# Gates applied on the way out of PSUM, and expert results summed by accumulating transfers, in a two-block MoE and hybrid-layer kernel

## The chip, the cores and the metric

One core of one Trainium2 chip runs the whole program in one launch. The metric is device time in microseconds (us), the median of several executions; the kernel before has 2867.81 us over three runs (2863.91 to 2868.19). The engines are called PE (matmul), PEld (weight load, beside PE), DVE, ACT, POOL and SP, as in the profile; each works through its own queue in order. SP's queue carries only transfers; POOL's and ACT's carry transfers beside their arithmetic.

## The reference

Two transformer blocks run one after the other on 512 tokens of width 1024. The first ends in a mixture of experts: each token goes to its 4 best of 32 experts, and the 4 results are weighted by softmax gates and summed. The second block is a hybrid layer (two attentions, a state-space branch, a gated convolutional feed-forward) which begins with a normalisation of the first block's output.

```python
gate = jax.nn.softmax(top_val, axis=-1)          # of the 4 best of 32 logits
def expert_block(args):
    gu = xblk @ w_gu[e] + b_gu[e]
    act = (up + 1.0) * (g * jax.nn.sigmoid(SWIGLU_ALPHA * g))   # after clamps
    return act @ w_down[e] + b_down[e]
out = zeros.at[tok_buf].add(yb * w_buf[:, None])               # w_buf: the gates
...
h = h + g2 * rmsnorm(ff, ffn_post_g)             # end of the first block
h = modulate(rms_norm(x, norm1), shift1, scale1) # start of the second
```

Since the gates of a token enter linearly, b_down can be summed apart, as gates times b_down, and each expert's result can be scaled by its gate at any place before the sum.

## The kernel before, in words

Every product is computed in three passes (each operand is split into a high and a low part), so that each 512 KB piece of weights is loaded by SP (`Stream.load`, L1541, tile `raw`), rounded by ACT (`hi`, L1566), subtracted by DVE or POOL (`lo`, L1568), and then streamed through PE (L1225 for the experts, L135 to L137 and L1719 elsewhere). Few `raw` buffers exist: SP's next load waits until DVE has read the buffer that it reuses.

The stages that the change touches, in order of time:

1. **Router** (`router`, L1025 to L1100, about 379 to 393 us). It computes ranks, gates G (128 x 4 x 32) and the table TW, which holds for each token and expert the four numbers that a slot of an expert's block must learn: token number (two columns), a one, and the token's choice number 0 to 3. At its end (L1096 to L1099) eight DVE instructions pick the four gates of each token into `k.gk`.
2. **Slots** (`make_slots`, L1150 to L1173). A one-hot matrix times TW puts the four numbers of each token into the slot that it has in the expert's block (L1162); DVE turns them into row numbers for the gather of the tokens (L1195) and for the scatter of the results (L1279). It runs for expert 0 first, and later for groups of up to four experts beside the experts' products. `further` (L1319) does the same for one block that is found at run time.
3. **Experts** (`experts`, `go_on`, about 410 to 1620 us). The loop over 32 experts is written out by hand for PE, ACT, DVE and POOL. For each of its 33 blocks of 128 rows, `out` (L1272) copies two 128 x 512 results from PSUM to `ey` on ACT (L1277), and POOL scatters the rows to `y_d` in HBM (L1279), at row 4 x token + choice.
4. **Middle** (`mid`, L2757 to L2802, about 1606 to 1686 us). PE multiplies the gates by b_down and ACT copies the sums to `xn` (L2779, L2780). Then for each of four token tiles: four fetches of 512 KB from `y_d` into `my` (L2786, on POOL's queue, 5 buffers), each added with its gate to `xn` by DVE (L2787); then the norm (ACT L2791, DVE L149, POOL L152, DVE L2793), the residual (DVE L2794), a store of it (POOL L2795), and the second block's norm (ACT L2796, POOL L152, ACT L2798). `run` (L2563) weaves this generator with `J.ctx`, the products of the 256 context tokens, whose weights come from `w_in` by SP; the numbers that the generators yield set how much of `J.ctx` is written between their steps.
5. **Turned** (`turned_g`, L1763). PE transposes the finished `xn` (L1770, four tiles into one bank, so that it needs all four), and then come the large products of the second block.

From the middle on, only the program order is written by hand; the framework lists each engine's instructions by when their inputs are ready in its own plan. The trace shows this: POOL issues the fetches of tile 1 before tile 0's power operation, which stands ahead of them in the program. On the chip each queue then runs in that fixed order.

Of the kernel before, what the change touches and what calls it, by code (L numbers as in the profile page):

```python
# [10 lines left out]
F32 = mybir.dt.float32  # L11
F32R = mybir.dt.float32r
BF16 = mybir.dt.bfloat16
I32 = mybir.dt.int32
AF = mybir.ActivationFunctionType
OP = mybir.AluOpType
AX = mybir.AxisListType
# [3 lines left out]
P = 128  # L21
D = 1024
T = 512
NT = T // P
# [5 lines left out]
TOPK = 4  # L30
# [994 lines left out]
def router(k, A, pool, lg, counted):  # L1025

    nc = k.nc
    TT = lambda o, a, b, op: nc.vector.tensor_tensor(o, a, b, op=op)
    E = NE
# [2 lines left out]
    ub = pool.tile([P, 2, P], BF16, name="ub")  # L1032
    nc.gpsimd.tensor_copy(ub[:, 0, :], k.C("upper"))
    nc.gpsimd.memset(ub[:, 1, :], 1.0)
    k.TW = k.mk.tile([P, NT, E, 4], BF16, name="TW")
    TW = k.TW
    nc.gpsimd.tensor_copy(TW[:, :, :, 0], k.C("p").unsqueeze(2).to_broadcast(sh))
    for t in range(NT):
# [11 lines left out]
    inc = pool.tile(sh, F32, name="rinc")  # L1050
# [15 lines left out]
    ps = sm_ps(k)  # L1066
# [14 lines left out]
    num = pool.tile(sh, F32, name="rnum")  # L1081
# [5 lines left out]
    G = pool.tile(sh, F32, name="G")  # L1087
# [5 lines left out]
    nc.vector.reciprocal(gs, gs)  # L1093
    TT(G, G, gs.unsqueeze(2).to_broadcast(sh), OP.mult)

    k.gk = lg[:, :, :TOPK]  # L1096
    for i in range(TOPK):
        nc.vector.scalar_tensor_tensor(inc, num, float(i), G, op0=OP.is_equal, op1=OP.mult)
        nc.vector.tensor_reduce(k.gk[:, :, i], inc, axis=AX.X, op=OP.add)  # L1099
    return G  # L1100


# [12 lines left out]
class Experts:  # L1115
# [34 lines left out]
    def make_slots(s, key, ranks, tw, n):  # L1150

        k, nc, pool = s.k, s.nc, s.pool
        oh = pool.tile([P, NT, n, P], BF16, name="oh", tag="oh", bufs=1)
        for t in range(NT):
            nc.vector.tensor_tensor(oh[:, t], s.iota.unsqueeze(1).to_broadcast([P, n, P]),
                                    ranks[:, t].unsqueeze(2).to_broadcast([P, n, P]), op=OP.is_equal)
            if t % 2:
                yield 1.5
        ps = sm_ps(k)
        for e in range(n):  # L1160
            for t in range(NT):
                nc.tensor.matmul(ps[:, e * 4:(e + 1) * 4], oh[:, t, e, :], tw(t, e), start=(t == 0), stop=(t == NT - 1))  # L1162
        yield 0.5
        sl = pool.tile([P, n, 4], F32, name="slots", tag="slots", bufs=2)
        nc.vector.tensor_copy(sl, ps[:, :4 * n].rearrange("p (e c) -> p e c", e=n))
        TT = lambda o, a, b, op: nc.vector.tensor_tensor(o, a, b, op=op)
        TT(sl[:, :, 0], sl[:, :, 0], sl[:, :, 1], OP.add)
        nc.vector.tensor_scalar(sl[:, :, 1], sl[:, :, 2], k.C("mdummy"), k.C("dummy"), op0=OP.mult, op1=OP.add)
        TT(sl[:, :, 1], sl[:, :, 1], sl[:, :, 0], OP.add)
        nc.vector.scalar_tensor_tensor(sl[:, :, 3], sl[:, :, 1], float(TOPK), sl[:, :, 3], op0=OP.mult, op1=OP.add)  # L1170
        idx = pool.tile([P, n, 2], I32, name="idx", tag="idx", bufs=3)
        nc.vector.tensor_copy(idx, sl[:, :, 1::2])
        s.groups[key] = [(idx[:, e, 0:1], idx[:, e, 1:2]) for e in range(n)]  # L1173

    def slots_g(s, i):

# [95 lines left out]
    def out(s, b, step=None):  # L1272
        nc = s.nc
        if step in (0, None):
            b.y = s.pool.tile([P, D], F32, name="ey", tag="ey", bufs=1)
            for n in range(2):
                nc.scalar.copy(b.y[:, n * 512:(n + 1) * 512], b.pd[n])  # L1277
        if step in (1, None):
            nc.gpsimd.indirect_dma_start(out=s.k.y_d[:, :], out_offset=bass.IndirectOffsetOnAxis(ap=b.slot[1], axis=0),  # L1279
                                         in_=b.y, in_offset=None, bounds_check=TOPK * T - 1, oob_is_err=False)  # L1280
# [38 lines left out]
    def further(s, i, b):  # L1319

        k, nc, pool = s.k, s.nc, s.pool
        TT = lambda o, a, b, op: nc.vector.tensor_tensor(o, a, b, op=op)
# [4 lines left out]
        oh = pool.tile([P, NE], F32, name="exoh", tag="exoh", bufs=1)  # L1327
# [4 lines left out]
        nc.vector.tensor_reduce(rk, tmp, axis=AX.X, op=OP.add)  # L1332
        nc.vector.tensor_scalar(rk, rk, ecol[:, 1:2], None, op0=OP.subtract)
        yield 1.0
        tw = pool.tile([P, NT, 4], BF16, name="extw", tag="extw", bufs=1)
        for c in range(4):
            TT(tmp, k.TW[:, :, :, c], oh.unsqueeze(1).to_broadcast(sh), OP.mult)
            with nc.allow_low_precision("one term is not zero"):
                nc.vector.tensor_reduce(tw[:, :, c:c + 1], tmp, axis=AX.X, op=OP.add)
# [449 lines left out]
class Block2:  # L1789
# [967 lines left out]
    def mid(s):  # L2757

        k, nc = s.k, s.nc
# [15 lines left out]
        for t in range(NT):  # L2775
            for n in range(2):
                c = slice(n * 512, (n + 1) * 512)
                ps = sm_ps(k)
                nc.tensor.matmul(ps, gT[:, t * P:(t + 1) * P], bd[:, c], start=True, stop=True)  # L2779
                nc.scalar.copy(s.xn[:, t, c], ps)  # L2780
        for t in range(NT):
            x, o = s.xn[:, t], slice(t, t + 1)
            rows = k.y_d[t * TOPK * P:(t + 1) * TOPK * P, :].rearrange("(p k) d -> p k d", k=TOPK)
            for i in range(TOPK):
                y = p.tile([P, D], F32, name="my", tag="my", bufs=5)
                nc.gpsimd.dma_start(y, rows[:, i])  # L2786
                nc.vector.scalar_tensor_tensor(x, y, k.gk[:, t, i:i + 1], x, op0=OP.mult, op1=OP.add)  # L2787
            yield 5.0
            h = hs[t]
            junk = p.tile([P, D], BF16, name="mjunk", tag="mjunk", bufs=1)  # L2790
            nc.scalar.activation(junk, x, AF.Square, accum_out=r[:, o])  # L2791
# [97 lines left out]
```

## Time and profile before

| | |
|---|---|
| median of 3 runs | 2867.81 us |
| the profiled execution, its own time | 2858.39 us |
| span of its trace | 2856.6 us |
| PE busy | 2688.8 us, 94% of the span |
| DVE busy | 2194.2 us, 77% |
| ACT busy | 1603.4 us, 56% |
| POOL busy | 666.5 us, 23% |

The profile's page gives the busy time of each engine over the span, then the span cut in 40 slices of 71.4 us with the busy share of each in tenths, the granted PE clock (9 or more in a slice is near its full rate), and the share that the 16 DMA engines were busy. Other views of the trace list instructions by line of the kernel with their durations, cut the span into stretches, follow the chain of work that ended last, and count the packets of each DMA queue: q0 is POOL's, q1 SP's and q10 ACT's. The trace's own execution is 9.4 us shorter than the median.

### The profile page before, as it was taken

The numbers are of one execution on the slowest core, as the hardware profiler recorded it, in microseconds if no ns is written. First come the engines' busy times: TensorE is split into PE (matmuls) and PEld (weight loads), VectorE is DVE, ScalarE is ACT, GpSimd is POOL, SyncE is SP. The second block draws the span as 40 slices with busy tenths as digits, with TensorE's granted clock in tenths as the row PEclk, the third lists the DMA queues.
The fourth block names the chain that finished last, engine by engine and source line by source line (L and its number), as shares of the span: only waits on it lengthen the run. The fifth ranks groups of instructions, "written<-read, shape, count | busy, mean of one in ns | idle before, by whom it ended". The sixth has DMA issues, their size and how long they took to land.

```text
span 2856.6 us, 37347 instructions
## 1 busy us (share of the span) xinstructions
PE 2688.8 (94%) x12897; PEld 2135.8 (75%) x12897; DVE 2194.2 (77%) x3210; ACT 1603.4 (56%) x2407; POOL 666.5 (23%) x472
## 2 busy tenths in 40 slices
PE   6789989999999999999999979999999999899998
PEld 2566748878888888888878667886688787688886
DVE  6998669999999999999999787767767555533312
ACT  3233347877777777777777564664456323433322
POOL 2664110122321001011100132003311432332222
PEclk8999889999999999999999989999999999999999
DMA  6555569999999999999999862221111664433232
GB/s 208 165 145 197 201 233 345 378 346 368 352 370 367 373 364 361 361 364 362 369 346 365 279 213 69 61 75 41 52 34 49 221 206 155 133 96 96 89 96 74
DMA packets 271743, 641.27 MB, mean 224 GB/s; under 512 B 53626, under 2 KB 99616, under 8 KB 271294
## 3 DMA queue, kind: packets, MB, share of 16 engines
q1 hardware_dynamic: 227440, 585.32, 58.5%
q0 software_dynamic: 13216, 30.17, 2.8%
q10 hardware_dynamic: 30894, 23.35, 2.7%
q8 instruction: 103, 1.69, 0.2%
q14 instruction: 90, 0.74, 0.1%
HBM read 622.30 MB, written 32.69 MB: 229 GB/s over the span
## 4 chain that ended last, share of the span: by engine, by line
PE 69%; DVE 9%; ACT 2%; issue 2%; DMA 1%; POOL 1%; ACTq 0%; SPq 0%; DVEq 0%; POOLq 0%
PE mm L1225 35%; PE mm L1719 6%; PE mm L135 4%; PE mm L137 4%; PE mm L136 4%; DVE lo L1568 3%; PE tr L221 2%; PE tr L1719 1%; PE sm L1719 1%; PE tr L2073 1%; PE mm L1232 1%; PE sm L135 1%; PE tr L135 1%; PE sm L2100 1%; PE sm L136 1%
## 5 line engine op out<-in xcount | busy, mean ns | idle before, releaser
L1568 DVE TENSOR_TENSOR lo<-raw,hi 128x1024 fp32r<-128x1024 f32 x938 | 1116.9, 1234 | 277.2 <-ACT hi L1566 275.7
L1566 ACT CAST hi<-raw 128x1024 fp32r<-128x1024 f32 x997 | 1014.8, 1056 | 478.1 <-PE mm L136 128.7
L1225 PE MATMUL mm<-hi,turnh 128*128 128x512 f32 x1584 | 508.1, 401 | 0.0
L1225 PE MATMUL mm<-hi,turnl 128*128 128x512 f32 x1584 | 498.4, 395 | 0.0
L1225 PE MATMUL mm<-lo,turnh 128*128 128x512 f32 x1584 | 497.9, 395 | 0.0
L1225 PEld LDWEIGHTS mm<-lo,turnh 128*128 128x128 f32 x1584 | 297.9, 188 | 71.4
L1225 PEld LDWEIGHTS mm<-hi,turnl 128*128 128x128 f32 x1584 | 297.8, 188 | 70.0
L1225 PEld LDWEIGHTS mm<-hi,turnh 128*128 128x128 f32 x1584 | 287.7, 188 | 57.9
L1279 POOL DMA_INDIRECT y_d<-ey,idx x33 | 95.4, 2890 | 969.8 <-ACT ey L1277 806.9
L1568 POOL TENSOR_TENSOR lo<-raw,hi 128x1024 fp32r<-128x1024 f32 (+1 forms) x59 | 145.4, 2465 | 554.0 <-ACT hi L1566 519.2
L141 ACT CAST turnh<-tr 128x512 fp32r<-128x512 f32 x132 | 77.5, 587 | 186.8 <-PE tr L221 186.8
L1654 DVE SCALAR_TENSOR_TENSOR mvacc<-mvw,silu_c,mvacc 128x512 f32<-128x512 f32 x112 | 103.1, 921 | 22.5 <-DMA mvw<-in_w_mod_dram 17.5
L135 PE MATMUL mm<-lhh,hi 128*128 128x512 f32 x288 | 118.0, 410 | 0.7 <-ACT apr L2061 0.7
L137 PE MATMUL mm<-lhh,lo 128*128 128x512 f32 x288 | 116.4, 406 | 0.0
L136 PE MATMUL mm<-lhl,hi 128*128 128x512 f32 x288 | 114.5, 398 | 0.0
L142 DVE TENSOR_TENSOR turnl<-tr,turnh 128x512 fp32r<-128x512 f32 x132 | 90.4, 685 | 9.0 <-ACT turnh L141 8.9
L2046 DVE TENSOR_REDUCE amax<-mm 128x1 f32<-128x256 f32 (+2 forms) x128 | 60.4, 501 | 39.5 <-PE mm L2041 21.1
L1719 PE MATMUL mm<-hi,lhh 128*128 128x256 f32 (+2 forms) x256 | 85.3, 336 | 4.3 <-DVE zt L2377 1.9
L2061 ACT ACTIVATE apr<-mm,negm 128x256 f32<-128x256 f32 (+2 forms) x128 | 68.7, 544 | 30.8 <-DVE negm L2051 16.4
L1719 PE MATMUL mm<-hi,lhl 128*128 128x256 f32 (+2 forms) x256 | 82.3, 324 | 2.3 <-POOL lhl L1784 2.3
L1719 PE MATMUL mm<-lo,lhh 128*128 128x256 f32 (+2 forms) x256 | 81.9, 320 | 1.0 <-DVE lo L1568 1.0
L135 PE MATMUL mm<-fhh,hi 128*128 128x512 f32 x192 | 77.4, 403 | 0.0
(756 smaller groups left out, 5173.5 us busy)
## 6 DMA issues: line engine op xcount, KB each, us to landing
raw<-in_exp_w_gu_dram SPq DMA_DIRECT2D x528, 512.0 KB
raw<-in_exp_w_down_dram SPq DMA_DIRECT2D x264, 512.0 KB
raw<-in_w_in_dram SPq DMA_DIRECT2D x83, 512.0 KB
mvw<-in_ada_w_dram SPq DMA_DIRECT2D x32, 512.0 KB
raw<-in_w_out_dram SPq DMA_DIRECT2D x32, 512.0 KB
mvw<-in_w_mod_dram SPq DMA_DIRECT2D x32, 512.0 KB
raw<-in_ffn_w_gate_dram SPq DMA_DIRECT2D x22, 512.0 KB
raw<-in_ffn_w_up_dram SPq DMA_DIRECT2D x22, 512.0 KB
```

Of the source, the lines that this page charges most:

```text
L135: k.nc.tensor.matmul(out, lh, rh, start=start, stop=False)
L136: k.nc.tensor.matmul(out, lh, rl, start=False, stop=False)
L137: k.nc.tensor.matmul(out, ll, rh, start=False, stop=stop)
L141: k.nc.scalar.copy(hi, src)
L142: k.nc.vector.tensor_tensor(lo, src, f(hi), op=OP.subtract)
L1225: nc.tensor.matmul(pss[n], a[:, j, :], c[:, n * 512:(n + 1) * 512], start=(j == 0 and i == 0), stop=(last and i == 2))
L1279: nc.gpsimd.indirect_dma_start(out=s.k.y_d[:, :], out_offset=bass.IndirectOffsetOnAxis(ap=b.slot[1], axis=0), in_=b.y, in_offset=None, bou ...
L1566: s.k.nc.scalar.copy(pm(hi[:, :m], True), pm(raw[:, :m], False))
L1568: eng.tensor_tensor(pm(lo[:, :m], True), pm(raw[:, :m], False), pm(f(hi[:, :m]), True), op=OP.subtract)
L1654: nc.vector.scalar_tensor_tensor(acc, v[:, j - q], sc(j), acc, op0=OP.mult, op1=OP.add)
L1719: k.nc.tensor.matmul(o, a[:, jj, sl], c[:, j, :], start=(jj == 0 and u == 0 and i % per == 0), stop=(jj == nk_all - 1 and u == 2), skip_gr ...
L2061: nc.scalar.activation(b.pr[:, o:o + n // P].rearrange("p a n -> p (a n)"), ps[:, :n], AF.Exp, bias=b.nm, scale=0.125, accum_out=tile_[t]. ...
```

## The change

The table TW grows from four to seven columns. The three new ones hold the gate, as three bf16 parts whose sum is the gate; the code that picked the gates into `k.gk` goes. The one-hot product hands the three parts to each slot, and two DVE additions put them together. `out` no longer copies from PSUM but applies the slot's gate as a per-row scale, so that `y_d` holds weighted rows. In `mid`, the 16 fetches no longer land in `my` but add to `xn` directly, and the 16 DVE instructions that scaled and added are gone. The fetches stand in the program in two halves: tiles 0 and 1 in turn, then tiles 2 and 3 in turn, all ahead of the loop over the tiles. Two additions to one tile must follow each other, since both read and write it.

```diff
@@ router
-    k.TW = k.mk.tile([P, NT, E, 4], BF16, name="TW")
+    k.TW = k.mk.tile([P, NT, E, 7], BF16, name="TW")
...
-    k.gk = lg[:, :, :TOPK]
-    for i in range(TOPK):
-        nc.vector.scalar_tensor_tensor(inc, num, float(i), G, op0=OP.is_equal, op1=OP.mult)
-        nc.vector.tensor_reduce(k.gk[:, :, i], inc, axis=AX.X, op=OP.add)
+    r = inc
+    nc.vector.tensor_copy(TW[:, :, :, 4], G)
+    TT(r, G, TW[:, :, :, 4], OP.subtract)
+    nc.vector.tensor_copy(TW[:, :, :, 5], r)
+    TT(r, r, TW[:, :, :, 5], OP.subtract)
+    nc.vector.tensor_copy(TW[:, :, :, 6], r)
@@ make_slots
-                nc.tensor.matmul(ps[:, e * 4:(e + 1) * 4], oh[:, t, e, :], tw(t, e), ...)
+                nc.tensor.matmul(ps[:, e * 7:(e + 1) * 7], oh[:, t, e, :], tw(t, e), ...)
-        sl = pool.tile([P, n, 4], F32, name="slots", tag="slots", bufs=2)
+        sl = pool.tile([P, n, 7], F32, name="slots", tag="slots", bufs=3)
...
+        TT(sl[:, :, 4], sl[:, :, 4], sl[:, :, 5], OP.add)
+        TT(sl[:, :, 4], sl[:, :, 4], sl[:, :, 6], OP.add)
+        s.groups[key] = [(idx[:, e, 0:1], idx[:, e, 1:2], sl[:, e, 4:5]) for e in range(n)]
@@ out
-                nc.scalar.copy(b.y[:, n * 512:(n + 1) * 512], b.pd[n])
+                nc.scalar.activation(b.y[:, n * 512:(n + 1) * 512], b.pd[n], AF.Copy, scale=b.slot[2])
@@ further
-        for c in range(4):
+        for c in range(7):
             TT(tmp, k.TW[:, :, :, c], oh.unsqueeze(1).to_broadcast(sh), OP.mult)
@@ mid
+        rows = k.y_d.rearrange("(t p k) d -> p t k d", p=P, k=TOPK)
+        for a in (0, 2):
+            for i in range(TOPK):
+                for t in (a, a + 1):
+                    nc.gpsimd.dma_start(s.xn[:, t], rows[:, t, i], accum_op=OP.add)
         for t in range(NT):
             x, o = s.xn[:, t], slice(t, t + 1)
-            for i in range(TOPK):
-                y = p.tile([P, D], F32, name="my", tag="my", bufs=5)
-                nc.gpsimd.dma_start(y, rows[:, i])
-                nc.vector.scalar_tensor_tensor(x, y, k.gk[:, t, i:i + 1], x, op0=OP.mult, op1=OP.add)
-            yield 5.0
+            yield 3.0
```

## Rows read from the trace of the kernel before

**Rows 1.** The page, part 2: the span in 40 slices of 71.4 us.

```profile
PE   6789989999999999999999979999999999899998
PEclk8999889999999999999999989999999999999999
```

**Rows 2.** Five stretches (us): busy us and count by engine, granted clock, DMA share, GB/s.

```profile
460.00:1600.00 1140.00, 1136.85 (x5275) 918.88 (x5273) 1121.84 (x1233) 881.31 (x1014) 172.95 (x76) 1.00 0.98 362
1626.00:1664.00 38.00, 28.32 (x148) 23.62 (x146) 29.85 (x53) 18.80 (x34) 18.24 (x26) 0.72 0.92 318
1664.00:1686.00 22.00, 16.69 (x112) 15.42 (x112) 21.29 (x33) 15.16 (x29) 5.41 (x7) 0.80 0.55 169
1686.00:1697.00 11.00, 8.66 (x61) 8.48 (x60) 8.34 (x21) 7.80 (x12) 0.00 (x0) 0.84 0.93 276
1697.00:1729.00 32.00, 24.00 (x139) 17.75 (x138) 27.99 (x38) 13.33 (x26) 17.47 (x13) 1.00 0.15 45
```

**Rows 3.** The chain of waits around the middle: start us, us, what.

```profile
1622.44 8.11 PE sm L2779 x12
...
1652.93 8.03 DMA raw<-in_w_in_dram
...
1664.52 4.30 DMA raw<-in_w_in_dram
```

**Rows 4.** Waits of SP's queue, 1600 to 1740 us: us in total, times, longest.

```profile
SPq L1541 <- DVE lo L1568: 112.4, 18, 22.5
```

**Rows 5.** The fetches and the additions by line: ns min/median/max, first and last start.

```profile
L2786 POOL DMA_DIRECT2D my<-y_d x16: 530/530/578, 1626.3 to 1658.2; - x16
DMA to landing us min/median/max: 4.2/5.7/7.4
L2787 DVE SCALAR_TENSOR_TENSOR xn<-my,lg,xn x16: 1273/1277/1285, 1630.9 to 1673.4; 128x1024 f32<-128x1024 f32 x16
```

**Rows 6.** DMA queues, 1626 to 1664 us: packets, MB, share of 16 engines.

```profile
q0 software_dynamic: 2736, 9.96, 71.8%
q1 hardware_dynamic: 4185, 2.11, 19.8%
```

**Rows 7.** The same, 1664 to 1697 us.

```profile
q1 hardware_dynamic: 6878, 3.95, 44.6%
```

**Rows 8.** Timelines of DVE, ACT and PE: the last tile's way to the transposes.

```profile
1673.43 1.28 DVE L2787 SCALAR_TENSOR_TENSOR xn<-my,lg,xn 128x1024 f32<-128x1024 f32 x1
...
1675.02 1.22 DVE L1568 TENSOR_TENSOR lo<-raw,hi 128x1024 fp32r<-128x1024 f32 x1
...
1684.44 1.15 ACT L2798 ACTIVATE xn<-mh,mq 128x1024 f32<-128x1024 f32 x1
...
1697.30 0.60 PE L1770 MATMUL tr<-ident,xn 128*128 128x128 f32 x4
```

**Rows 9.** The router's instructions, by line and on the timelines.

```profile
L1098 DVE SCALAR_TENSOR_TENSOR rinc<-rnum,G x4: 278/284/293, 387.8 to 391.4; 128x128 f32<-128x128 f32 x4
387.46 0.27 DVE L1028 TENSOR_TENSOR G<-G,gsum 128x128 f32<-128x128 f32 x1
386.56 0.22 PE L1162 MATMUL sm<-TW,oh 128*128 128x4 bf16 x2
391.81 1.29 POOL L1195 DMA_INDIRECT xg<-xn_d,idx  x1 [17.17 <-DVE rinc L1098]
398.35 0.88 PE L221 MATMUL tr<-identr,xg 128*128 128x128 f32 x8
410.05 0.61 PE L1109 MATMUL tr<-ident,G 128*32 128x128 f32 x2 [7.85 <-SPq L1400]
```

**Rows 10.** By line: a slot addition's kin, ACT without and with a per-row scale, the PSUM copy.

```profile
L1170 DVE SCALAR_TENSOR_TENSOR slots<-slots x10: 151/168/170, 390.4 to 1493.2; 128x4 f32<-128x4 f32 x7, 128x1 f32<-128x1 f32 x2, 128x3 f32<-128x3 f32 x1
L2796 ACT ACTIVATE xn<-mh x4: 1053/1057/1060, 1643.1 to 1681.8; 128x1024 f32<-128x1024 f32 x4
L2798 ACT ACTIVATE xn<-mh,mq x4: 1132/1150/1153, 1646.6 to 1684.4; 128x1024 f32<-128x1024 f32 x4
L1277 ACT COPY ey<-mm x66: 580/590/597, 461.7 to 1620.4; 128x512 f32<-128x512 f32 x66
```

More of the change, by code (lines that the diff above doesn't have):

```diff
@@ L1161, in make_slots @@
             for t in range(NT):
-                nc.tensor.matmul(ps[:, e * 4:(e + 1) * 4], oh[:, t, e, :], tw(t, e), start=(t == 0), stop=(t == NT - 1))
+                nc.tensor.matmul(ps[:, e * 7:(e + 1) * 7], oh[:, t, e, :], tw(t, e), start=(t == 0), stop=(t == NT - 1))
         yield 0.5
-        sl = pool.tile([P, n, 4], F32, name="slots", tag="slots", bufs=2)
-        nc.vector.tensor_copy(sl, ps[:, :4 * n].rearrange("p (e c) -> p e c", e=n))
+        sl = pool.tile([P, n, 7], F32, name="slots", tag="slots", bufs=3)
+        nc.vector.tensor_copy(sl, ps[:, :7 * n].rearrange("p (e c) -> p e c", e=n))
         TT = lambda o, a, b, op: nc.vector.tensor_tensor(o, a, b, op=op)
@@ L1171, in make_slots @@
         idx = pool.tile([P, n, 2], I32, name="idx", tag="idx", bufs=3)
-        nc.vector.tensor_copy(idx, sl[:, :, 1::2])
-        s.groups[key] = [(idx[:, e, 0:1], idx[:, e, 1:2]) for e in range(n)]
+        nc.vector.tensor_copy(idx, sl[:, :, 1:4:2])
+        TT(sl[:, :, 4], sl[:, :, 4], sl[:, :, 5], OP.add)
+        TT(sl[:, :, 4], sl[:, :, 4], sl[:, :, 6], OP.add)
+        s.groups[key] = [(idx[:, e, 0:1], idx[:, e, 1:2], sl[:, e, 4:5]) for e in range(n)]
     def slots_g(s, i):
@@ L1334, in further @@
         yield 1.0
-        tw = pool.tile([P, NT, 4], BF16, name="extw", tag="extw", bufs=1)
-        for c in range(4):
+        tw = pool.tile([P, NT, 7], BF16, name="extw", tag="extw", bufs=1)
+        for c in range(7):
             TT(tmp, k.TW[:, :, :, c], oh.unsqueeze(1).to_broadcast(sh), OP.mult)
@@ L2780, in mid @@
                 nc.scalar.copy(s.xn[:, t, c], ps)
+        rows = k.y_d.rearrange("(t p k) d -> p t k d", p=P, k=TOPK)
[3 more added lines that the diff above has]
+                    nc.gpsimd.dma_start(s.xn[:, t], rows[:, t, i], accum_op=OP.add)
         for t in range(NT):
             x, o = s.xn[:, t], slice(t, t + 1)
-            rows = k.y_d[t * TOPK * P:(t + 1) * TOPK * P, :].rearrange("(p k) d -> p k d", k=TOPK)
-            for i in range(TOPK):
-                y = p.tile([P, D], F32, name="my", tag="my", bufs=5)
-                nc.gpsimd.dma_start(y, rows[:, i])
-                nc.vector.scalar_tensor_tensor(x, y, k.gk[:, t, i:i + 1], x, op0=OP.mult, op1=OP.add)
-            yield 5.0
+            yield 3.0
             h = hs[t]
```

## The prediction

> **What bounds the kernel now.** I first read the slices of the page [rows 1]: PE stands at 9 nearly throughout, and one notch, at slice 23 (1643 to 1714 us), lies in the part that the change rebuilds. Next the stretches [rows 2]. From 460 to 1600 us PE is busy 1136.85 of 1140 us; DVE, with 1121.84, is close behind, and ACT, with 881.31, has room. In the middle it is different: from 1626 to 1697 us PE is busy 53.7 of 71 us, at a granted clock of 0.72 to 0.84. Of the two levels (1.2 and 2.4 GHz) the low one shows only in such stretches with gaps. What the middle costs stands there, and so does what the change can give or take.
>
> Two resources share the middle. From 1626 to 1664 us the DMA engines are 0.92 busy; from 1664 to 1686 us DVE is busy 21.29 of 22 us and the DMA only 0.55 [rows 2]. The chain of waits says the same: weight loads of `w_in` hold the end at 1652.93 us for 8.03 us and at 1664.52 us for 4.30 us [rows 3]. SP's queue, for its part, waits 112.4 us in 18 waits for `lo` on DVE, to get buffers back [rows 4]. So the fetches of expert results press on the weight loads first, and the additions on DVE press on them second. The change lightens the second and may make the first heavier.
>
> **Part 1, router.** Eight DVE instructions go and five of the same size come. What moves is an edge: the first slot product reads all of TW, so it must now wait for the gates. It started at 386.56 us, while G was ready at 387.46 + 0.27 = 387.73 us [rows 9]. Five more, each starting some 0.2 us after the last (L1098 is 0.28 us long and overlaps), end near 388.9 us: the product comes 2.4 us later. Six of the eight that go stood in the way of the row numbers, 1.2 us. So the gather, at 391.81 us, is some 1.2 us late. Behind it wait the transposes of its rows at 398.35 us, and POOL has nothing else queued there; PE then sits 7.85 us behind a barrier until 410.05 us [rows 9]. How early the rows landed is not shown, so the price lies between 0 and 2.4 us; I take 0.5, since 6.5 us lie between issue and use.
>
> **Part 2, slots.** Ten calls of two additions at 0.168 us [rows 10] make 3.4 us of DVE; `further` adds six instructions like L1098, 1.7 us. All of this lies beside the experts, where DVE has 18 us left in 1140 and PE 3 [rows 2]. Cover: DVE's gaps; without them it would cost 5.1 us. I take 1 us. The product of seven columns instead of four is too short to count. A third `slots` buffer takes away the wait that the longer life would make.
>
> **Part 3, gates on ACT.** A per-row scale costs 1150 - 1057 = 93 ns [rows 10], so the 66 copies of 0.59 us grow by 6.1 us in all. ACT is idle for 259 us of that stage [rows 2], and nothing waits 0.09 us for a bank there. Only the last block's two, 0.2 us, stand before the last scatter. I take 0, and without the cover 6.
>
> **Part 4, the additions on DVE go.** 16 x 1.277 us = 20.4 us [rows 5]. Where DVE is not the limit (1626 to 1664 us, busy 29.85 of 38) that gives nothing. Where it is, four of them lie between 1668 and 1674.7 us, 5.1 us, and ahead of the `lo` at 1675.02 us [rows 8], for which SP's loads wait; the DMA is idle for 0.45 x 22 = 9.9 us in that stretch [rows 2]. So the gain lies between 5.1 us and 9.9 us.
>
> **Part 5, the fetches add.** No row shows such a transfer. The nearest is the plain fetch. POOL's queue moved 2736 packets in 71.8% of 16 x 38 us, 0.160 us each [rows 6]; the 16 fetches are 16 x 128 of them, 327 us on 16 engines, or 20.4 us. The lower end is that adding costs nothing more; below that I see no way, since the same bytes must come. The upper end is that the target row must be read as well, one more packet read for each: another 20.4 us. I take the upper end, because the sum cannot be made without reading `xn`, and the DMA has no copy of it.
>
> The Trainium skill, in *Collectives: The Full Stack*, section "The bandwidth ceiling: the fold count and why AG ≠ RS ≠ AR", says that a transfer that reduces reads two sources on the same read ring and so runs at half the rate, the addition itself being free. That speaks against this change: by it the sum is the one below, and by the plain fetch's row it would be the first rival's, 8 us faster than before. No trace here shows it.
>
> Now the order. Before, the last fetch was issued at 1658.2 us and landed by about 1664 us [rows 5]. With 20.4 us more in a stretch that had 0.08 x 38 = 3 us free, the last addition lands near 1681 us. Counting waits gives the same: an addition must wait for the one before it on its tile; with two tiles in turn that makes eight rounds of two issues (1.06 us) and a landing (5.7 us), 54 us from 1626.3, or 1680 us. The last tile then needs what it needs today from its last addition to its finished `xn`, 1674.7 to 1685.6 us, 10.9 us [rows 8], and some 2 us more as two tiles end together: about 1694 us. The transposes began at 1697.3 us [rows 8], so `xn` itself is not late.
>
> Late next are the weight loads. Until 1664 us SP got 2.11 MB through beside the fetches; the remaining 3.95 MB then took until 1697 us, 33 us [rows 6, 7]. With POOL's queue holding the DMA for 55 us instead of 38, of which it uses (2048 x 0.32 + 688 x 0.16) / 16 = 48, SP's 0.029 us packets (19.8% of 608 us over 4185) get 7 us, the same 2 MB as before. The same 33 us thus start at 1681 us instead of 1664, 17 us late, less the 9.9 us in which the DMA had stood idle for want of DVE (Part 4, its upper end, since DVE has no additions left at all): **7 us later**.
>
> **Sum.** 0.5 + 1 + 0 + 7 = 8.5 us more. Against the profiled execution: 2858.4 + 8.5 = 2866.9 us. The median stands 9.4 us above that execution, so the forecast for the median is 2876.3 us, rounded to 2876.
>
> **Rivals.**
>
> *Plain price (faster).* The adding transfer costs what the plain one does. Then the loads start as today, and DVE gives back 9.9 us, less 1.5: 8 us faster, 2860. At worst it is 5.1 less 1.5, 4 us; at best all 20.4 us count, less 1.5: 19 us, since the tiles then land before DVE was through with them. For it: the DMA's share is time in packets, and the second read may lie beside the first. Against it: the DMA is already at 0.92 there [rows 2]. It decides if the packets of the change stay near 0.16 us.
>
> *Rounds and POOL (much slower).* Price and wait add up: a round is 1.06 + 5.7 us plus the doubled time of two transfers, 2 x 128 x 0.16 / 16 = 2.6 us; eight rounds of 9.3 us end at 1701 us, `xn` is ready at about 1714 instead of within 1697, so 17 us plus 1.5: 2886. POOL runs in order, so whatever is queued behind a waiting addition waits too: the power operations of the norms and of the context keys (DVE and then PE's transposes wait for them), the loads of the residual, the stores. It decides if the second pair is issued only when the first is through. Against it: POOL's list is made by readiness, so all four tiles may be in flight at once, and then the waits overlap.
>
> *Hidden.* The DMA's 14 idle us between 1626 and 1697 [rows 2] take up nearly all of the added 20.4, and the time ends within 2 us of today, 2868 to 2870. In this case the change does not do what it says it does for DVE either: the relief comes where nobody waits for DVE.
>
> **How the numbers follow.** About 0.2% of the time, 5.7 us, is what a measurement of this kernel can tell from no change. Forecast 0.40, plain price 0.28, rounds 0.17, hidden 0.15. The forecast's own range is 2 to 14 us slower (its ends: DVE's relief at 5.1 us and Parts 1 to 3 uncovered, or one read of the two half hidden); three quarters of it lie beyond 5.7 us. Slower: 0.30 + 0.17 = 0.47. Faster: the plain price but for its low end, 0.23, and 0.04 of the hidden case, should DVE's relief reach the stretch from 1697 us on, where DVE is busy 27.99 of 32 us [rows 2]: 0.27. The rest, 0.26, is no difference. The range takes in the middle of the plain price and the rounds: 2857 to 2889.
>
> **What would show it.** Right: 16 adding transfers whose packets take near 0.32 us; the last landing near 1680 us on today's clock; DVE with gaps in the middle; `w_in` loads in the chain of waits up to the transposes; the experts' stage of the same length within 1 us; ACT at 0.68 us per 512 columns. Wrong: packets near 0.16 us, or a middle that ends before 1697 us; or POOL's power operations in the chain, which is the rounds' mark.

## The result, and the profile after

The changed kernel takes 2891.54 us (median of 5 runs, 2882.72 to 2895.31) against 2867.54 us for the kernel before (5 runs): a ratio of 1.0084, 95% interval 1.0065 to 1.0102. It is **24 us slower**. The forecast was 2876 us, 8.5 us slower, with a range up to 2889: the direction was right, the size was not, and the time lies above the range. The profiled execution took 2890.16 us.

The page's slices (part 2 of the page, after), to be laid beside [rows 1]:

```profile
PE   6788889999999999999999849999999999899998
PEclk8899989999999999999999969999999999999999
```

Behind the start there is still one notch, at slices 22 and 23 (counted from 0, as in the prediction), and it is deeper: 8 and 4 instead of 9 and 7. Everything that follows is about it. I measure it from the start of the last scatter to the start of the first transposes of the finished `xn`, and call that **the stretch**. Its ends, by line, before and then after:

```profile
L1279 POOL DMA_INDIRECT y_d<-ey,idx x33: 991/1423/10817, 463.1 to 1621.2; - x33
...
L1770 PE MATMUL tr<-ident,xn x32: 272/273/328, 1697.3 to 1718.5; 128*128 128x128 f32 x32
```

```profile
L1283 POOL DMA_INDIRECT y_d<-ey,idx x33: 996/1832/10617, 471.6 to 1630.8; - x33
...
L1774 PE MATMUL tr<-ident,xn x32: 272/273/328, 1728.2 to 1751.3; 128*128 128x128 f32 x32
```

The scatter starts 9.6 us later, of which 7.1 us lie ahead of the router's ranking, where both kernels issue the same instructions in the same order. The ranking begins behind four maxima of the logits (L1045); the last one, before and then after:

```profile
L1045 DVE MAX8 m<-lg x4: 195/195/196, 347.4 to 378.9; 128x8 f32<-128x32 f32 x4
```

```profile
L1045 DVE MAX8 m<-lg x4: 194/194/195, 356.7 to 386.0; 128x8 f32<-128x32 f32 x4
```

Over all kernels below it came between 372 and 387 us without pattern, so I take this for chance. From that last maximum to the first expert's product it is 33.6 us instead of 32.2; from there to the last scatter 1211.2 instead of 1210.1; the stretch is **97.4 us instead of 76.1**; from the transposes to the end 1160.1 instead of 1159.3. The sum of these differences, 1.4 + 1.1 + 21.3 + 0.8 = 24.6 us, agrees with the medians.

The stretch in windows of the whole of it (columns as in [rows 2]), before and then after:

```profile
1621.20:1697.30 76.10, 57.53 (x326) 49.24 (x327) 60.71 (x106) 45.15 (x78) 24.66 (x33) 0.78 0.80 263
```

```profile
1630.80:1728.20 97.40, 53.72 (x302) 47.23 (x301) 41.09 (x88) 42.84 (x74) 25.21 (x33) 0.70 0.83 197
```

DVE did get its relief: 41.09 us busy instead of 60.71. The DMA engines are as busy as before as a share (0.83 and 0.80), but in a stretch that is 21 us longer, and they move 197 instead of 263 GB/s. The DMA queues of the same two windows (packets, MB, share of 16 engines), before and then after:

```profile
q0 software_dynamic: 3312, 11.72, 42.1%
q1 hardware_dynamic: 12827, 6.96, 33.5%
```

```profile
q0 software_dynamic: 3312, 11.72, 55.4%
q1 hardware_dynamic: 12003, 6.13, 23.7%
```

POOL's queue moves the same 3312 packets and takes 0.554 x 97.4 = 54.0 us of all engines for them, where it took 0.421 x 76.1 = 32.0: **22 us more DMA time**. The idle time of the DMA stays at 0.17 x 97.4 = 16.6 us (before 0.20 x 76.1 = 15.2). So none of the new DMA time went into the gaps, and the stretch grew by all of it. While the additions are in flight (1638 to 1672 us, to be laid beside [rows 6]) the packets of the two queues look like this:

```profile
q0 software_dynamic: 1598, 5.83, 90.9%
q1 hardware_dynamic: 2077, 1.05, 13.2%
```

A packet of POOL's queue takes 0.909 x 544 / 1598 = 0.309 us instead of 0.160, with the same mean size (3.65 and 3.64 KB); the forecast took 0.32. Both means hold packets of 4 bytes too. Of the 4 KB packets of POOL's queue in the stretch, taken one by one from the trace, the median takes 0.327 us, and before 0.159: a factor of 2.06. The figure of 0.28 us in the later expectations came from a window that began ahead of the additions. The Trainium skill, in *Collectives: The Full Stack*, section "The bandwidth ceiling: the fold count and why AG ≠ RS ≠ AR", says of the transfers of ring collectives that one that reduces runs at half the rate. The trace agrees, with 0.327 us against 0.159.

The additions by line, the waits of SP's queue from 1600 to 1760 us, and the chain of waits in the middle, after:

```profile
L2790 POOL DMA_DIRECT2D xn<-y_d x16: 860/876/1237, 1635.7 to 1689.0; - x16
...
  DMA xn<-y_d: 25.5, 8
...
DMA to landing us min/median/max: 6.2/8.3/10.7
```

```profile
SPq L1545 <- DVE lo L1572: 78.4, 19, 23.1
```

```profile
1645.22 33.07 DMA raw<-in_w_in_dram
...
1685.54 7.92 DMA xn<-y_d
```

An addition takes 8.3 us to land instead of 5.7, and 0.876 us to issue instead of 0.530 [rows 5]. The chain had waits of 8.03 and 4.30 us for weights [rows 3]; now it has one of 33.07 us, and then one for an addition. SP waits less for DVE, 78.4 instead of 112.4 us [rows 4]: what is late is now the transfer itself. POOL's timeline shows what happens to the last three additions:

```profile
1669.75 0.88 POOL L2790 DMA_DIRECT2D xn<-y_d  x1 [3.80 <-DMA xn<-y_d]
1680.84 0.58 POOL L152 TENSOR_TENSOR mr<-mr,mhalf 128x1 f32<-128x1 f32 x1 [10.21 <-DVE mr L149]
...
1682.06 0.90 POOL L2790 DMA_DIRECT2D xn<-y_d  x1
1684.03 1.55 POOL L152 TENSOR_TENSOR mr<-mr,mhalf 128x1 f32<-128x1 f32 x1 [1.07 <-DVE krms L1963]
1685.54 0.88 POOL L2790 DMA_DIRECT2D xn<-y_d  x1
...
1689.04 0.86 POOL L2790 DMA_DIRECT2D xn<-y_d  x1 [2.07 <-DMA xn<-y_d]
```

They stand behind the power operation of tile 0 (L152), which waits for DVE, which waits for ACT, whose queue has a `hi` of the late weight load ahead of the square sum (`mjunk`):

```profile
1678.39 1.04 ACT L1570 CAST hi<-raw 128x1024 fp32r<-128x1024 f32 x1 [9.99 <-DMA raw<-in_w_in_dram]
1679.34 1.05 ACT L2796 ACTIVATE mjunk<-xn 128x1024 bf16<-128x1024 f32 x1
```

So two suspects are in view, and they are tangled: the price of the additions in DMA time, and the queue on POOL. The sums are late as well, by the last step of `xn`:

```profile
L2803 ACT ACTIVATE xn<-mh,mq x4: 1132/1137/1152, 1695.6 to 1709.7; 128x1024 f32<-128x1024 f32 x4
```

It ends at 1710.9 us, 80.1 us after the last scatter instead of 64.4 (to 1685.6 us, [rows 8]), and the transposes follow 17.3 us later (before 11.7), behind context products on PE.

### The profile page after: what moved, and what is told of

Read it like the earlier page. It is cut to its first block, busy times and chain, and to the rows that moved or that the text cites. A ratio compares the mean times of both kernels' runs of the same rounds, so it can differ in the third digit from the quotient of the medians.

```text
span 2888.3 us, 37335 instructions
## 1 busy us (share of the span) xinstructions
PE 2693.6 (93%) x12897; PEld 2139.2 (74%) x12897; DVE 2181.3 (76%) x3217; ACT 1606.8 (56%) x2407; POOL 680.9 (24%) x472
## 4 chain that ended last, share of the span: by engine, by line
PE 68%; DVE 9%; ACT 3%; DMA 2%; issue 2%; POOL 1%; DVEq 0%; ACTq 0%; SPq 0%; POOLq 0%
PE mm L1229 34%; PE mm L1723 6%; PE mm L135 4%; PE mm L137 4%; PE mm L136 4%; DVE lo L1572 4%; PE tr L221 1%; DMA raw<-in_w_in_dram 1%; PE tr L1723 1%; PE sm L1723 1%; PE tr L2077 1%; PE mm L1236 1%; PE sm L135 1%; PE sm L2104 1%; PE tr L135 1%
## 5 line engine op out<-in xcount | busy, mean ns | idle before, releaser
L1283 POOL DMA_INDIRECT y_d<-ey,idx x33 | 112.3, 3404 | 952.3 <-ACT ey L1281 709.7
```

## The experiments

Eighteen kernels were run. The expectations are quoted as they were written, with the names that the theories had at that time. In the later ones they are four: **S**, the weight loads starve because their packets are small; **Q**, POOL's in-order queue holds the additions up; **D**, the adding packets simply take DMA time that the loads share; **L**, additions to one tile follow each other one landing at a time. Each kernel has a ratio to the kernel before (its own runs of it, 95% interval in brackets) and the length of the stretch in its profile.

**Either half of the change.** e1 keeps the gates on ACT and fetches and adds as before; e2 has the adding transfers and no gates at all.

```diff
# e1, on the changed kernel
...
-                    nc.gpsimd.dma_start(s.xn[:, t], rows[:, t, i], accum_op=OP.add)
...
+                y = p.tile([P, D], F32, name="my", tag="my", bufs=5)
+                nc.gpsimd.dma_start(y, rows[:, i])
+                nc.vector.tensor_tensor(x, x, y, op=OP.add)
# e2, on the kernel before: the opposite, in mid alone
```

> All of the change but the middle: ACT applies the gates, TW has seven columns, and the middle fetches into its five buffers as before, with a plain DVE addition (1.22 us instead of 1.28) for each. Theory M (the whole loss is in the middle: the adding transfers): within 3 us of before. Theory R (part of the loss is the router and the slots, since the changed kernel's first expert product began 8.4 us later): 6 to 10 us slower than before.

> The middle alone: before, with the 16 adding transfers in place of fetch and DVE addition; no gates are applied anywhere, so each token's four results are summed unweighted. Theory M: 20 to 30 us slower than before, as the changed kernel. Theory R: 12 to 18 us.

e1: 1.003 [1.0015, 1.0044], 8.6 us slower, as theory R had it; stretch 78.3 us. e2: 1.0097 [1.0069, 1.0125], 28 us slower, as theory M had it; stretch 100.5 us. The two add up to more than the change, so the times can't be divided that finely. By the stretches, the loss there comes with the adding transfers, and the gates cost something of their own, more than forecast.

**More DMA time without adding.** e3 is the kernel before with every fetch issued twice, the second copy unread.

```diff
+                y2 = p.tile([P, D], F32, name="my2", tag="my2", bufs=2)
+                nc.gpsimd.dma_start(y2, rows[:, i])
```

> Before, with each of the 16 fetches made twice, the second into a buffer that nobody reads (and four landing buffers instead of five): as many packets as the adding transfers are worth by their doubled packet time, but no transfer waits for the one before on its tile. Theory C (load on the DMA engines starves the weight loads, nothing else): 15 to 25 us slower, as the changed kernel. Theory W (waits of the adding transfers and what is queued behind them on POOL and ACT): under 10 us slower.

1.0054 [1.0029, 1.0079]; stretch 90.9 us, 14.8 longer. The queue of POOL in that stretch:

```profile
q0 software_dynamic: 5616, 20.11, 60.7%
```

That is 0.607 x 90.9 = 55.2 us, as much as in the changed kernel (54.0), with no addition. The time is 15.5 us longer, at the lower edge of theory C (15 to 25). More DMA time without adding brings two thirds of the 21 us, though not quite alone: POOL has 16 more transfers to issue, and waits 12.8 us in 6 waits (L2788) for a landing before it can use an unread buffer again.

**The changed kernel again.**

> The changed kernel once more, for a second profile. If the 7 us by which its router began late belong to the change, they are there again; if they are chance, the router's first maximum is again near 378.9 us as before. The middle from the last scatter to the first transposes again takes near 98 us (before 76).

1.0099 [1.0071, 1.0127], stretch 97.6 us: the result holds. The router's last maximum came at 372.4 us here, 13.6 us sooner than in the first profile.

**Wider rows of weights.** f1 and f2 load ten of the context weights' pieces with rows of 1 KB instead of 512 B, in the changed kernel and in the one before.

```diff
-        w = 256 if want_y else 128
+        w = 256
```

> The changed kernel, but the state-space weights of the context tokens are loaded 256 columns wide instead of 128, in rows of 1 KB instead of 512 B (the same bytes, half the packets). Theory S (the weight loads starve: one short packet of theirs passes for each adding packet of 0.28 us): the 33 us wait for a weight load falls to under 18 us and the stretch from the last scatter to the first transposes from 97 to under 88 us, so some 10 us faster than the changed kernel, 12 to 18 us slower than before. Theory Q (additions stand on POOL's queue behind a power operation that waits for ACT): no more than 4 us gained.

> The kernel before with the same wider loads. Theory S: its two waits for weight loads in the middle (8.03 and 4.30 us) shrink, 3 to 8 us faster than before. If the weight loads were no limit there: within 2 us.

f1: 1.0094 [1.0069, 1.0118], stretch 98.0 us. f2: 1.0028 [1.0014, 1.0042], stretch 82.5 us, which neither theory had. The changed kernel gains nothing by wider rows, and the kernel before loses 6 us by them. The chain of f1 still waits 29.66 us for one load.

**Another order on POOL.** f3 takes all four tiles in turn, so that every addition stands ahead of the power operations; f5 keeps POOL in program order.

```diff
# f3
-        for a in (0, 2):
+        for a in (0,):
             for i in range(TOPK):
-                for t in (a, a + 1):
+                for t in range(NT):
# f5
-        weave(middle, J.ctx, rate=0.6)
+        with s.k.tc.manual_schedule(engines={mybir.EngineType.Pool}):
+            weave(middle, J.ctx, rate=0.6)
```

> The changed kernel with the additions in turn over all four tiles instead of two pairs. All 16 then stand on POOL's queue ahead of any power operation, and up to four are in flight. Theory Q: the last addition is issued some 12 us sooner after the last scatter (58 us in the changed kernel), and the time falls 8 to 15 us below the changed kernel's. Theory S: the loads starve as before, so it stays within 5 us of the changed kernel although the sums are ready sooner.

> The changed kernel with POOL's queue in program order through the middle: all 16 additions in their pairs, then the power operations; nothing else is changed. Theory Q: the ten idle us of POOL before the fourteenth addition go, and the time falls 8 to 12 us below the changed kernel's. Theory S: within 5 us of the changed kernel.

f3: 1.011 [1.0084, 1.0136], stretch 102.3 us. Its additions and its chain of waits:

```profile
L2790 POOL DMA_DIRECT2D xn<-y_d x16: 863/874/1557, 1628.2 to 1667.8; - x16
```

```profile
1635.73 24.52 DMA raw<-in_w_in_dram
...
1662.66 19.34 DMA raw<-in_w_in_dram
```

The last addition is issued 44.5 us after the last scatter instead of 58.2, and the kernel is no faster: the weights are late by as much more. f5 goes the other way: 1.0139 [1.0115, 1.0164], stretch 115.1 us; there the context keys' power operations wait behind all additions until 1711 us. POOL's queue can make things worse, but clearing it mends nothing. Q alone falls.

**The same bytes in whole rows.** g2 and g3 load each such piece as 128 rows of 4 KB.

```diff
+        whole = s.nl in s.whole and nk * n <= w.shape[1]
+        if whole:
+            s.k.nc.sync.dma_start(raw[:, :nk * n], w[k0 * P:(k0 + 1) * P, :nk * n])
...
```

> The changed kernel, with each 512 KB piece of the context tokens' weights loaded as 128 rows of 4 KB from the same matrix instead of 1024 rows of 512 B: the same bytes, the same instructions behind them, but the wrong weights (so the context products of the second block's branch are not the reference's). To be read beside g3, which does the same to the kernel before. Theory S (the adding packets of about 0.28 us take the DMA engines packet by packet in turn with SP's, so that SP's small packets get 31 instead of 55 GB/s while the additions are in flight): with rows of 4 KB SP gets eight times the bytes in each turn, the waits for `raw` in the chain shrink from 33 us to under 15, and the stretch from the last scatter to the transposes is within 10 us of g3's instead of 21 us longer. Theory Q (POOL's additions stand behind its power operations, which stand behind DVE and ACT): rows of weights change nothing in that queue's order, but the queue waits for late loads only in part, so the last addition is still issued 55 us or more after the last scatter and the stretch stays 15 us or more longer than g3's.

> The kernel before, with the same pieces loaded as 128 rows of 4 KB (wrong weights, as in g2). Theory S: the loads finish sooner beside the fetches, too; the stretch from the last scatter to the transposes shortens from 76 us to 65 to 72, DVE then being what is late there, and the time falls by 4 to 10 us. Theory Q: no loads were late because of their rows, so the time stays within 4 us of the kernel before.

g2: 1.0079 [1.005, 1.0107], stretch 95.2 us. g3: 0.9991 [0.997, 1.0013], stretch 77.4 us. They lie 17.8 us apart, and 10 at most was what S asked for. The late loads did leave the chain, but additions took their place; the five waits for an addition in g2's chain there, 47.6 us in all:

```profile
1639.99 13.13 DMA xn<-y_d
1653.40 9.49 DMA xn<-y_d
...
1663.71 9.13 DMA xn<-y_d
1673.13 7.09 DMA xn<-y_d
1680.73 8.80 DMA xn<-y_d
```

So S falls as well. Both numbers that Q had named for g2 did come (17.8 us apart, and the last addition 55.5 us after the last scatter), but not for Q's reason: the waits of POOL between the additions are for landings,

```profile
  DMA xn<-y_d: 34.7, 10
```

and no wait for a power operation lies among them. f3 and g2 together are the lesson: make the sums sooner and the weights are late, make the weights sooner and the sums are late. Both stand in the same DMA time. That is theory D, so far argued; h1 and h4 test it.

**What DVE's relief is worth.** g1 is e1 with DVE's additions cut to one column; g4 is e1 with one addition in four on POOL.

```diff
# g1, on e1
-                nc.vector.tensor_tensor(x, x, y, op=OP.add)
+                nc.vector.tensor_tensor(x[:, :1], x[:, :1], y[:, :1], op=OP.add)
# g4, on e1
+                (nc.gpsimd if i == 1 else nc.vector).tensor_tensor(x, x, y, op=OP.add)
```

> The kernel of e1 (gates on ACT, plain fetches), with DVE's 16 additions cut to one of their 1024 columns: the fetches keep their price and the additions on DVE are all but gone, as the change would have it if adding in the transfer were free (this leaves out nearly all of the sum over the experts). It measures Part 4 alone. If DVE's additions bind the middle: 5 to 10 us faster than e1, last scatter to transposes 68 to 73 us instead of 78. If the loads bind it beside the fetches anyway: within 3 us of e1.

> The kernel of e1 with one of the four additions of each tile on POOL instead of DVE: a candidate that would take 5 us off DVE without an adding transfer. If DVE binds the middle as Part 4 has it: 2 to 5 us faster than e1. If the loads bind it, or POOL's slower additions delay its own fetches: no gain, or up to 5 us slower than e1.

g1: 0.9989 [0.9972, 1.0005], stretch 75.2 us, 3.1 shorter than e1's. By the ratios g1 lies 11.7 us below e1 (some 5 to 18, from the two intervals), so the two measures of DVE's relief don't agree here. g4: 1.0044 [1.0026, 1.0061], stretch 85.9 us: an addition takes 2426 ns on POOL and 1216 ns on DVE, and the sum waits for it.

**Without the loads.** h1 and h2 split 11 of the context pieces from one tile that is loaded once; for this the middle's buffers are freed later in both.

```diff
+        if s.nl in s.whole and s.one is not None:
+            s.raw[s.nl] = s.one
+            s.nl += 1
+            return True
...
```

> The changed kernel, with 11 of the context tokens' loads of 512 KB left out: their pieces are split from one tile that is loaded once (wrong weights for the context tokens; ACT's and DVE's work on the pieces stays). That takes some 20 us of DMA time out of the stretch between the last scatter and the transposes, which is 97 us long. Theory D (the additions' packets hold the DMA engines 22 us longer, and sums and weights share that time): the stretch falls by 12 us or more, to 85 or less. Theory L (additions on one tile follow each other one landing at a time, and POOL's queue holds the rest up, whatever else the DMA does): the landings set the end with or without loads, and the stretch stays above 90 us.

> The kernel before, with the same 11 loads left out. Theory D: its DMA was idle for 15 of 76 us, so less is to be gained than in h1: the stretch falls by 0 to 10 us (DVE, busy for 61 of 76 us, comes next), and h1 comes within 16 us of it. Theory L: the stretch falls by as much as in h1 or more, and the distance stays at 21 us or more.

h1: 1.0055 [1.0037, 1.0073], stretch 85.3 us, 12.1 shorter than the changed kernel's; that is at the edge of what D asked for (12 or more, to 85 or less). h2: 1.0017 [1.0, 1.0033], stretch 77.2 us, 1.1 longer. The two now lie 8.1 us apart instead of 21.3. Taking the loads out of the DMA brings the changed kernel 12 us and the kernel before nothing: that is the sharing which D says, and not L, by which the landings would have set the end with or without loads. What is left, 8 us, would then be the additions' own way.

**The price of adding alone.** h4 makes the 16 fetches of the kernel before adding transfers, but into five zeroed spare tiles, from which DVE adds as before. The five memsets take 4.5 us of POOL right behind the last scatter, mostly while it lands: the first fetch starts 5.5 us after the scatter instead of 5.1.

```diff
...
-                y = p.tile([P, D], F32, name="my", tag="my", bufs=5)
-                nc.gpsimd.dma_start(y, rows[:, i])
+                y = ys[(t * TOPK + i) % 5]
+                nc.gpsimd.dma_start(y, rows[:, i], accum_op=OP.add)
```

> The kernel before, with its 16 fetches made adding transfers, but into five zeroed spare tiles in turn, from which DVE still adds as before (so the sums hold other rows too; the output isn't the reference's). The price of adding alone: five are in flight, none waits for another on its tile but through a spare tile's reuse, and POOL's order stays that of before. Theory D: packets near 0.28 us, the stretch from the last scatter to the transposes 88 to 98 us, the time 12 to 22 us above before. Theory L: the price alone is hidden; within 6 us of before.

1.0076 [1.005, 1.0102], 22 us slower; stretch 93.8 us, 17.7 longer than before. POOL's queue while the additions run (1632 to 1676 us), and over the stretch:

```profile
q0 software_dynamic: 2246, 8.22, 92.2%
...
q0 software_dynamic: 3312, 11.72, 56.3%
```

0.922 x 704 / 2246 = 0.289 us a packet, with plain stores and fetches of POOL among them (the median of the 4 KB packets in the stretch is 0.328 us), and 0.563 x 93.8 = 52.8 us in the stretch. No chain of additions on a tile but through a spare tile's reuse, POOL's fetches and power operations interleaved as before, DVE with all its additions: and most of the loss is there. **The price of the adding transfers is the main cause**; their longer issue on POOL (0.923 us, plain 0.530) is part of it in h4, and was not measured apart.

**More work on DVE.** h3 is the kernel before with each addition on DVE followed by one that nobody reads.

```diff
+                nc.vector.scalar_tensor_tensor(y, y, k.gk[:, t, i:i + 1], x, op0=OP.mult, op1=OP.add)
```

> The kernel before, with each of DVE's 16 additions followed by one more of the same size that nobody reads (20.4 us more of DVE in the middle). It doubles what Part 4 took away. If DVE binds the middle as Part 4 has it (10 us of relief for 20 us of work): 10 to 20 us slower than before, last scatter to transposes 86 to 96 us. If DVE's additions lie beside the loads: under 5 us slower.

1.0071 [1.0049, 1.0092], 20 us slower; stretch 89.7 us, 13.6 longer. So 20 us more on DVE cost 14 in the stretch.

**The two terms still open.** i1 is the kernel before with its additions cut to one column; i2 is e1 with ACT copying instead of scaling.

```diff
# i1, on the kernel before
-                nc.vector.scalar_tensor_tensor(x, y, k.gk[:, t, i:i + 1], x, op0=OP.mult, op1=OP.add)
+                nc.vector.scalar_tensor_tensor(x[:, :1], y[:, :1], k.gk[:, t, i:i + 1], x[:, :1], op0=OP.mult, op1=OP.add)
# i2, on e1
-                nc.scalar.activation(b.y[:, n * 512:(n + 1) * 512], b.pd[n], AF.Copy, scale=b.slot[2])
+                nc.scalar.copy(b.y[:, n * 512:(n + 1) * 512], b.pd[n])
```

> The kernel before, with DVE's 16 additions cut to one of their 1024 columns (this leaves out nearly all of the sum over the experts): Part 4's relief on its own, against the kernel before itself. By Part 4's upper end 9.9 us faster, by its lower end 5.1 us; by the stretch that e1 and g1 showed (78.3 and 75.2 us) 3 us faster, with a stretch of 72 to 75 us.

> The kernel of e1 (gates in the slots, plain fetches and additions on DVE), with ACT copying from PSUM as before instead of scaling (this leaves out the gates). It splits what e1 lost over before (8.6 us, 4.3 to 12.6). If ACT's scale costs it, Part 3: within 3 us of before. If the router's edge and the slots' instructions cost it, Parts 1 and 2: 5 to 10 us slower than before, with the experts' stage at 1212 us as in the kernels with gates rather than at 1208.

i1: 0.999 [0.9975, 1.0005], about 3 us; stretch 73.5 us, 2.6 shorter than before:

```profile
1624.70:1698.20 73.50, 56.63 (x332) 48.98 (x331) 44.10 (x106) 45.50 (x78) 20.57 (x33) 0.84 0.84 274
```

DVE has 16.6 us less to do there (44.10 against 60.71) and the stretch gives 2.6 of them; by the times it is 2.9 us, between 7.2 faster and 1.4 slower. i2: 1.004 [1.0025, 1.0055], no faster than e1, so ACT's scale is not what e1 lost by.

## Why the prediction was right and where it failed

**Part 3, gates on ACT: right.** 92 ns a copy (93 forecast), and it costs nothing that shows, by i2:

```profile
L1281 ACT ACTIVATE ey<-mm,slots x66: 677/682/693, 470.0 to 1629.9; 128x512 f32<-128x512 f32 x66
```

**Parts 1 and 2, router and slots: too small.** Forecast 0.5 + 1 us. The eleven kernels that hand the gates through the slots take 33.3 us on average from the router's last maximum to the first product (32.6 to 34.1), the nine others 31.9 (31.3 to 33.6): 1.4 us, inside the bounds of 0 to 2.4. From there to the last scatter it is 1212.5 us on average (1210.6 to 1215.1) against 1208.7 (1206.6 to 1210.6): 3.8 us where 1 was taken. The work itself was counted right; the slots' additions of two columns, from 380 to 1620 us, before and then in i2:

```profile
L1166 DVE TENSOR_TENSOR slots<-slots 128x4 f32<-128x4 f32 (+2 forms) x20 | 3.3, 165 | 0.5
```

```profile
L1168 DVE TENSOR_TENSOR slots<-slots 128x4 f32<-128x4 f32 (+2 forms) x40 | 6.6, 169 | 0.9
```

20 more, 3.3 us (3.4 forecast). What failed was the cover: a DVE with 18 us free in 1140 hid little of it, and the bound of 5.1 us was nearer than 1. Together about 5 us instead of 1.5. By the ratios of e1 and i2, 8.6 and 11.5 us, it may be more; by g1 and i1, which leave DVE's additions out with and without the gates (0.9989 and 0.999), it may be nothing. That difference stays open. In the pair of profiles of the result it is 2.5 us.

**Part 5, the price of the adding transfers: right.** The upper end was taken because `xn` must be read as well. 0.309 us a packet (0.327 for 4 KB alone) instead of 0.32, 22 us more DMA time over the stretch instead of 20.4, the loads behind: h4's stretch is 17.7 us longer with that price, where the forecast had "17 us late". That the two agree so closely is in part luck, since the sums did not end where Part 5 had them: "so `xn` itself is not late" came out wrong. On the clock of before (9.6 us off) `xn` was done at 1701.3 us, not at 1694, and so behind the 1697.3 us at which the transposes had begun; in h4, too, it came 17 us later after the scatter than before. The *plain price* rival falls by the packets, and *hidden* by the DMA's idle time, which stayed.

**The step that failed** is the next one in Part 5: "less the 9.9 us in which the DMA had stood idle for want of DVE (Part 4, its upper end, since DVE has no additions left at all): 7 us later". It read an idle DMA beside a busy DVE [rows 2] as time that comes back once DVE is free. i1 measures that relief by itself: 2.6 us of the stretch, under both ends of Part 4 (5.1 and 9.9). Its times (2.9 us, at most 7.2) leave the lower end open and speak against the upper one; only g1 against e1 (3.1 us by the stretch, 11.7 by the ratios) could still be read as more. The DMA's slices over the stretch (tenths busy, 40 slices), before and in i1, show where it went:

```profile
DMA  5885899999789699999997759800029769998879
```

```profile
DMA  7898999998699989999999999997508069755078
```

The hole of before, four slices with 0, 0, 0 and 2, closes when DVE's additions are gone, as the forecast had it; but new ones open behind it, where the norms of the last tiles and the context's products follow, and the idle time as a whole is still 0.16 x 73.5 = 11.8 us of 15.2. And beside the adding price nothing of it is left: h4, whose DVE does all its additions, has a stretch of 93.8 us, and the changed kernel, whose DVE does none, 97.4. How much of that is a small relief, and how much a relief that the waits of one addition for another ate up, only their difference shows.

h3 shows why this was easy to misjudge: 20 us added on DVE cost 13.6, so DVE does stand near the end, and [rows 8] are no illusion. But taking work from it gives 2.6, since the loads are nearly as late: in i1's chain of waits one of them follows where the additions had stood. (A run without both was not made.)

```profile
1661.53 12.15 DMA raw<-in_w_in_dram
```

What a longer DVE costs here is not what a shorter one gives back.

**The rest.** 17.7 (h4) less 2.6 (i1) leaves 6.2 us of the 21.3. This is what the *rounds and POOL* rival named: additions on one tile wait for each other, 25.5 us in 8 waits on POOL, and the last three stand behind a power operation. That POOL's order can cost so much is shown (f5: 18 us more); that exactly these 6.2 us are its share follows from the subtraction only, and from a relief taken beside plain fetches, and f3, which cleared the queue, got nothing back, as the loads were then late. This rival's number, 2886, was nearer to the result than the forecast, but its mechanism is not the main one: in h4 the 16 transfers, which wait for each other only through a spare tile's reuse, still take 44 us to issue (1632.3 to 1676.3), where the plain fetches took 32 [rows 5] and the changed kernel's 53; POOL's queue alone holds the DMA engines 92.2% of that time.

On the chain on a tile the Trainium skill, *DMA: Bandwidth & Descriptors*, section "🎯 Rules for kernel authors", says that an accumulating transfer reads its destination first and writes it later with nothing holding the bytes in between, so the next one must wait for the earlier one's semaphore. The trace agrees that this wait is paid: the 25.5 us above.

The range has a slip of its own: with the terms named for its upper end (relief at 5.1 us, Parts 1 to 3 uncovered) the sum is 17 - 5.1 + 2.4 + 5.1 + 6 = 25 us, not 14. That would have taken in the result, but by Parts 1 to 3 at 13.5 us, where the runs show about 5.

So the account, from one profile of each kernel (the two profiles of the changed one have 97.4 and 97.6 us), is 17.7 - 2.6 + 6.2 in the stretch, 2.5 for router, slots and experts, 0.8 behind the transposes: 24.6 us, where the forecast had 17 - 9.9 + 1.5, rounded to 8.5.

**A better version** was not found. i1 and g1 leave nearly all of the additions out and fetch at the plain price: 0.999 [0.9975, 1.0005] and 0.9989 [0.9972, 1.0005]. Even a sum that cost neither DVE nor DMA time beyond these fetches would hardly be seen here, so the kernel before stays the faster one.

## What to carry to other kernels

Before an operation is moved into a transfer, ask whether the DMA engines have time in that very stretch: an adding transfer took twice the packet time of a plain one here (0.327 against 0.159 us for 4 KB), and beside loads that share the engines nearly all of it came out at the end. Idle time of one resource beside a busy other one is not a gain to be booked: leave the work out in a run and see what the stretch gives back. And when one remedy makes the sums sooner and the weights later, and another the reverse, look for the resource that both share.

## What was not expected of the hardware

Longer rows of weights did not help the time: with 1 KB rows (f2) the kernel before was 0.28% slower [0.14, 0.42], and with 4 KB rows (g3) it was the same. Yet they did get more through while adding packets fill the engines: SP's queue has 13.2% from 1638 to 1672 us in the changed kernel, 15.9% from 1635 to 1669 us in f1 and 23.9% from 1637 to 1672 us in g2 (1.05, 1.58 and 2.70 MB). g2 is no faster by it, since its chain waits for additions instead. And in h2, taking 5.3 MB of loads out of the stretch did not shorten it at all, though loads of weights stood in its chain of waits [rows 3]: the sums and their norms were just as late.
